# Norms of the differential attention: transposed on TensorE and stored as rows of 128 queries

## The chip, the cores and the metric

The kernel runs on one core of a Trainium2 chip. The metric is the device time of one execution in microseconds (us); three runs of the kernel before gave 2115.82, 2119.69 and 2121.97, so the median is 2119.69 us.

A core has five engines with a queue of instructions each: PE (TensorE, matrix products and transposes), DVE (VectorE), ACT (ScalarE), POOL (GpSimd) and SP (SyncE, which here only issues transfers). An engine works through its queue in order. They meet through semaphores: an instruction whose input isn't ready waits, and what is queued behind it on its engine waits with it.

## The reference

One layer is computed for two sequences (1024 and 2048 tokens): a modulated projection, a windowed attention (half A), a differential attention (half B), an output projection and a layer norm. The change concerns the norm of half B, an RMS norm over the 128 elements of each head:

```python
def rms_norm(x, w):
    xf = x.astype(jnp.float32)
    y = xf * lax.rsqrt(jnp.mean(jnp.square(xf), -1, keepdims=True) + SUBLN_EPS) * w.astype(jnp.float32)
    return y.astype(x.dtype)

def diff_attention(q, k, v, lq1, lk1, lq2, lk2, subln_w, rel_bias, lambda_init):
    ...
        p = jax.nn.softmax(logits + bias[None, :, None], axis=-1)
        w = p[:, :, 0] - lam * p[:, :, 1]
        return jnp.einsum('bhqk,bkhe->bqhe', w.astype(vh.dtype), vh)
    ...
    o = rms_norm(o, subln_w) * (1.0 - lambda_init)
```

For each of 4 heads and each query there is one number 1/sqrt(mean square + eps). The output projection needs it beside the head's output.

## The kernel before

The stages overlap: projections (50 to 1142 us), windowed attention among them (668 to 1045), the differential attention (its logits from 1076 to 1801), and the output stage (from 1829 to the end). The change lies in the differential attention and the first part of the output stage.

**Units, groups and slots.** The long sequence (s = 1) comes first, head by head, then the short one (s = 0). A unit is a block of queries of one head: 128 queries with all 2048 keys in the long sequence, 256 queries with 1024 keys in the short one. A group is 256 queries: two units of the long sequence, one unit of the short one. There are 80 units and 48 groups (32 long, 16 short), numbered from 0 here. `slot(n)` writes the work of one time step n, in four steps j = 0 to 3. In each step PE gets, in this order: four matmuls of logits of unit n (L826), six matmuls of values of an older group (L882 to L884), four transposes of the probabilities of unit n - 3 (L864). In one step of a slot `square_sum` (j = 1) adds two transposes (L897).

**What happens to logits.** DVE adds the bias and takes the minimum (L831), ACT takes the exponential with a sum (L839), DVE forms the factor of the second softmax (L841, L844), POOL scales one of the two rows (L848, two instructions a unit) and adds the other (L850, two). This combined row is what PE transposes three slots later; ACT and DVE copy the transposed block out of PSUM as a high and a low part (L866, L867). The PSUM blocks for transposes are two buffers named `tp`, used in turn.

**The norm.** `square_sum(g)` transposes a group's output (L897), ACT squares and sums it (L899), DVE adds eps times the squared sum of the softmax (L903), POOL raises it to the power -1/2 (L905). The result is `f[:, 4:6]`: 128 partitions (queries) by 2 blocks. A small function `store` is put on the list `stores`; it writes these 256 numbers to the row `frow[s][h, ...]` in device memory, one element from each of 128 partitions, twice. One `store` is taken from the list in each step while n < N = 80, and only in step j = 0 after that. In the output stage `load_rest` reads `frow` back with one row for all 128 partitions (L1024), and POOL multiplies the heads' outputs with it (L1034).

**What sets the order.** In the differential attention only PE's queue is written by hand (`manual_schedule(engines={PE})`): it is the order of the code in `slot`. The queues of the other engines are set by a scheduler at build time. In the output stage all queues are in the order of the code. W (L757, L759) is the bias of a head: it is loaded by SP and widened by two POOL instructions a head ahead of its use.

Of the kernel before, what the change touches and what calls it, by code (L numbers as in the profile page):

```python
# [11 lines left out]
F32 = mybir.dt.float32  # L12
# [8 lines left out]
P = 128  # L21
# [46 lines left out]
def hybrid_layer(ctx, tc, x_prompt, x_sample, c_prompt, c_sample, w_in, w_out, w_ada, b_ada, ln_g, ln_b,  # L68
                 attn_sink, lambda_q1, lambda_k1, lambda_q2, lambda_k2, subln_w, rel_bias, oh, eye,
                 y_prompt, y_sample):  # L70
    nc = tc.nc
# [3 lines left out]
    def pool(stack, name, bufs=1, space=None, side=None):  # L75
        if space is None:
            return stack.enter_context(tc.tile_pool(name=name, bufs=bufs, side=side, reuse_waits="tile"))
        if space == DRAM:
            return stack.enter_context(tc.tile_pool(name=name, bufs=bufs, space=space))
        return stack.enter_context(tc.tile_pool(name=name, bufs=bufs, space=space, side=side, reuse_waits="tile"))  # L80
# [6 lines left out]
    def tp():  # L87
        return ps_tp.tile([P, 512], F32, tag="tp", name="tp")
# [4 lines left out]
    def dt_(shape, name):  # L93
        return dram.tile(shape, F32, name=name, tag=name)
# [15 lines left out]
    frow = [dt_([HB, S], f"frow{s}") for s, S in enumerate(SEQS)]  # L110
    tbl = dt_([HA + HB, P, NREL], "tbl")

    ident = const.tile([P, P], F32, name="ident")
# [274 lines left out]
    def fill(n):  # L388
        for _ in range(n):
            next(steps, None)  # L390
# [316 lines left out]
    class Views:  # L707
# [5 lines left out]
        def next(self):  # L713
            if len(self.made) < self.count:
                self.made.append(self.make())
            self.n += 1
            return self.made[(self.n - 1) % self.count]

    SMAX = max(SEQS)
    QG = 256  # L720
# [6 lines left out]
    for s in (1, 0):  # L727
        T = SEQS[s] // P
        for h in range(HB):
            for i in range(0, T, 2):  # L730
                g = len(groups_of)
                n = len(units)
# [6 lines left out]
    N = len(units)  # L739
# [5 lines left out]
    st, lst = ExitStack(), ExitStack()  # L745
# [40 lines left out]
    def prefetch(n, j):  # L786

        s, h, i, g = units[n]
        if j == 1:
            for u in units[n + 1:n + (3 if n >= EARLY - 1 else 2)]:  # L790
                if u[3] == asked[0] + 1 and (u[0] == 0 or u[3] == units[n + 1][3]):
                    load_queries(u[3])
        if n in staged and j == 2:
            stage(staged[n])
        if i == (4 if s else 2) and j == 2 and (s, h) != units[-1][:2]:
            load_head(*next_head[s, h])
        if n + 1 < N and units[n + 1][2] == 0 and j == 3:
            load_keys(*units[n + 1][:2], range(2, SEQS[units[n + 1][0]] // CH))
# [53 lines left out]
    def transpose(n, j):  # L852
        s, h, i, g = units[n]
        b, kq = (i % 2, j) if s else divmod(j, 2)
        qs = slice(b * P, (b + 1) * P)
        if j == i == 0:
            load_values(s, h)
        if b == 0:
            groups_[g]["PT"].append((pt_p.tile([P, 4, QG], F32R, tag="pth", name="pth"),
                                     pt_p.tile([P, 4, QG], F32R, tag="ptl", name="ptl")))  # L860
        H, L = groups_[g]["PT"][kq]
        pt = tp()
        for c in range(4):
            nc.tensor.transpose(pt[:, c * P:(c + 1) * P], rows[n][0][:, (j * 4 + c) * P:(j * 4 + c + 1) * P], ident)  # L864
        p3 = pt.rearrange("p (j q) -> p j q", j=4)
        nc.scalar.copy(H[:, :, qs], p3)  # L866
        nc.vector.tensor_tensor(out=L[:, :, qs], in0=p3, in1=H[:, :, qs].bitcast(F32), op=ALU.subtract)  # L867
        if j == 3:
            del rows[n]

    def values(g, piece):
        s, h, i = groups_of[g]
        T = SEQS[s] // P
        G = groups_[g]
        Vt = heads[s, h][2]
        if piece == 0:
            G["O"] = ac()
        a = G["O"][:, :QG]
        for kb in range(piece * 2, piece * 2 + 2):
            kq, c = divmod(kb, 4)  # L880
            H, L = G["PT"][kq]
            nc.tensor.matmul(a, lhsT=Vt[kq][:, 0, c, :], rhs=H[:, c, :], start=(kb == 0), stop=False)  # L882
            nc.tensor.matmul(a, lhsT=Vt[kq][:, 0, c, :], rhs=L[:, c, :], start=False, stop=False)  # L883
            nc.tensor.matmul(a, lhsT=Vt[kq][:, 1, c, :], rhs=H[:, c, :], start=False, stop=(kb == T - 1))  # L884
        if piece == T // 2 - 1:
            osb = e_p.tile([P, QG], F32, tag="osb", name="osb")
            nc.scalar.copy(osb, a)
            (nc.sync if now[0] < N else nc.scalar).dma_start(out=OT[s][h][:, i * P:i * P + QG], in_=osb)
            G["osb"] = osb

    def square_sum(g):
        s, h, i = groups_of[g]
        G = groups_[g]
        ss = st_p.tile([P, 2], F32, tag="ss", name="ss")
        ot = [G["O"][:, QG + b * P:QG + (b + 1) * P] for b in range(2)]
        for b in range(2):
            nc.tensor.transpose(ot[b], G["osb"][:, b * P:(b + 1) * P], ident)  # L897
        for b in range(2):
            nc.scalar.activation(ot[b], ot[b], AF.Square, accum_out=ss[:, b:b + 1])  # L899
        f = st_p.tile([P, 6], F32, tag="f", name="f")  # L900
        nc.scalar.activation(f[:, 0:2], G["s0"], AF.Square, scale=EPS ** 0.5)
        for b in range(2):
            nc.vector.tensor_scalar(out=f[:, 2 + b:3 + b], in0=ss[:, b:b + 1], scalar1=1.0 / P,  # L903
                                    scalar2=f[:, b:b + 1], op0=ALU.mult, op1=ALU.add)
        nc.gpsimd.tensor_tensor(out=f[:, 4:6], in0=f[:, 2:4], in1=mhalf, op=ALU.pow)  # L905
        del groups_[g]

        def store():
            nc.sync.dma_start(out=frow[s][h, i * P:i * P + QG].rearrange("(b p) -> p b", p=P), in_=f[:, 4:6])

        stores.append(store)

    now, stores = [0], []

    def slot(n, extra, other=None):
        now[0] = n
        for j in range(4):
            if extra:
                fill(extra)
            if n < N:  # L920
                logits(n, j)
                prefetch(n, j)
            for g, piece in values_at.get(n, ()):
                if piece % 4 == j:
                    values(g, piece)
            if 0 <= n - LAG < N:
                transpose(n - LAG, j)
            if j == 1 and n in sums_at:
                square_sum(sums_at[n])
            if stores and (n < N or j == 0):  # L930
                stores.pop(0)()
            if other is not None:
                next(other, None)

    st_p = pool(st, "stat", 8, side="right")
    for r in (k_p, q_p, wb_p, r1_p, r0_p):
        r.open(st, "right")
    ps_lg.open(lst, space=PSUM)
    with tc.manual_schedule(engines={PE}):
        for n in range(EARLY):  # L940
            slot(n, 5)
        project_until(2, 13)
    pst.close()
    pt_p = pool(st, "pt", 7)
    v_p = pool(st, "vq", 5)
    e_p = pool(st, "e", 2)
    for r in (r0_p, r1_p, wb_p, k_p, q_p):
        r.open(st)
    ps_lg.open(lst, space=PSUM)
# [199 lines left out]
    with tc.manual_schedule(engines={PE}):  # L1149
        for n in range(EARLY, N):  # L1150
            slot(n, 0)
# [3 lines left out]
    with tc.manual_schedule(engines=ENGINES):  # L1155
        for n in range(N, max(sums_at) + 1):
            slot(n, 0, other)
        for store in stores:
            store()
        for _ in other:  # L1160
            pass
# [27 lines left out]
```

## Time and profile before

| | us |
|---|---|
| median of 3 runs | 2119.69 |
| the profiled execution's own time | 2119.7 |
| its span, first to last instruction | 2117.9 |
| PE busy | 2065.7 (98%) |
| DVE busy | 1299.6 (61%) |
| POOL busy | 1150.9 (54%) |
| ACT busy | 1039.7 (49%) |
| mean granted clock of PE | 0.994 of full |

The shares are means over stages with different limits, so the stage of the change is read by itself below. "Busy" of PE is a modelled figure: consecutive matmuls overlap, and the spacing of their starts tells what one costs. In the page's last section the store of the norms is `frow<-f`, 48 issues of 1.0 KB.

### The profile page before, as it was taken

Reading aid. Unit: us, or ns where it says so; the run is one execution under the profiler, and the core shown is the slowest. Engines: PE = TensorE matmul, PEld = TensorE weight load, DVE = VectorE, ACT = ScalarE, POOL = GpSimd, SP = SyncE. Lnnn points to the kernel's source line nnn. Section 1 sums busy time; section 2 is a strip of 40 time slices with the busy share of each in tenths; the row PEclk is TensorE's granted clock in tenths of the full one; section 3 lists DMA queues with packets and bytes.
Section 4 is the critical chain, followed back from the end, with each engine's and each line's share of the span. In section 5 each row is a group of like instructions: output and inputs, shape, how many; then the busy total and the mean of one; then the engine's idle time right before and its main releaser. Section 6 shows DMA issues by size and latency. Waiting matters only on the chain.

```text
span 2117.9 us, 32626 instructions
## 1 busy us (share of the span) xinstructions
PE 2065.7 (98%) x11597; PEld 1776.0 (84%) x11597; DVE 1299.6 (61%) x2536; ACT 1039.7 (49%) x2022; POOL 1150.9 (54%) x830
## 2 busy tenths in 40 slices
PE   7999999999999999999999999999999998799998
PEld 4777898888988888888897999999999988688886
DVE  6334224222225777777654999999999988555555
ACT  5211113011015767777623777777777887522221
POOL 3213213212224344334353889898898889577774
PEclk9999999999999999999999999999999999899999
DMA  9685635435538868778454133132231496767763
GB/s 274 183 289 156 188 121 169 131 124 134 154 118 225 207 166 217 203 198 210 131 164 146 48 91 78 39 104 58 82 78 47 114 158 87 164 157 194 197 196 103
DMA packets 340203, 312.46 MB, mean 148 GB/s; under 512 B 32086, under 2 KB 296950, under 8 KB 339656
## 3 DMA queue, kind: packets, MB, share of 16 engines
q1 hardware_dynamic: 339320, 309.72, 54.4%
q8 instruction: 92, 1.51, 0.4%
q14 instruction: 71, 0.58, 0.2%
q10 hardware_dynamic: 720, 0.66, 0.1%
HBM read 212.70 MB, written 97.60 MB: 147 GB/s over the span
## 4 chain that ended last, share of the span: by engine, by line
PE 86%; DMA 7%; DVE 3%; POOL 2%; issue 1%; ACT 1%; SPq 1%; DVEq 0%; POOLq 0%; ACTq 0%
PE lg L826 13%; PE pj L187 12%; PE pj L188 12%; PE pj L189 12%; PE tp L864 6%; PE po L1069 4%; PE po L1071 4%; PE po L1070 4%; PE ac L884 3%; PE ac L883 3%; PE ac L882 3%; PE lgA L608 3%; PE tp L644 3%; PE ac L636 2%; DMA Q<-qb 1%; PE ac L635 1%
## 5 line engine op out<-in xcount | busy, mean ns | idle before, releaser
L187 PE MATMUL pj<-uH,wH 128*128 128x512 f32 x1040 | 418.4, 402 | 4.7 <-DVE gg L258 4.7
L189 PE MATMUL pj<-uH,wL 128*128 128x512 f32 x1040 | 407.5, 392 | 0.0
L218 POOL TENSOR_TENSOR wL<-wr,wH 128x1024 fp32r<-128x1024 f32 x74 | 181.8, 2459 | 415.0 <-DVE wH L216 374.1
L188 PE MATMUL pj<-uL,wH 128*128 128x512 f32 x1040 | 407.0, 391 | 0.0
L826 PE MATMUL lg<-kt,Q 128*128 128x512 f32 x1280 | 376.4, 416 | 9.2 <-DMA Q<-qb 6.2
L850 POOL TENSOR_TENSOR l<-l,l 128x1024 f32<-128x1024 f32 x160 | 382.9, 2414 | 1.2
L839 ACT ACTIVATE l<-l,nm 128x2048 f32<-128x2048 f32 (+1 forms) x192 | 330.9, 1723 | 19.0 <-DVE nm L831 18.9
L826 PEld LDWEIGHTS lg<-kt,Q 128*128 128x128 f32 x1280 | 217.6, 190 | 40.7 <-issue 6.7
L831 DVE CUSTOM_DVE_ANT_0 l<-lg,W 128x1024 f32<-128x1024 f32 x192 | 233.4, 1215 | 11.6 <-PE lg L826 8.7
L866 ACT CAST pth<-tp 128x512 fp32r<-128x512 f32 x320 | 186.0, 581 | 108.2 <-PE tp L864 97.1
L189 PEld LDWEIGHTS pj<-uH,wL 128*128 128x128 f32 x1040 | 195.5, 188 | 42.5
L187 PEld LDWEIGHTS pj<-uH,wH 128*128 128x128 f32 x1040 | 195.9, 188 | 37.6 <-DVE gg L258 5.6
L848 POOL TENSOR_SCALAR l<-l,s 128x1024 f32<-128x1024 f32 x160 | 178.8, 1130 | 82.3 <-PE lg L826 45.4
L867 DVE TENSOR_TENSOR ptl<-tp,pth 128x512 fp32r<-128x512 f32 x320 | 209.2, 685 | 21.9 <-ACT pth L866 20.5
L188 PEld LDWEIGHTS pj<-uL,wH 128*128 128x128 f32 x1040 | 196.3, 189 | 31.0
L864 PE MATMUL tp<-ident,l 128*128 128x128 f32 x1280 | 193.6, 274 | 7.1 <-DVE ptl L867 7.1
L623 POOL TENSOR_SCALAR l<-l,rcA 128x384 f32<-128x384 f32 (+1 forms) x144 | 81.0, 581 | 190.7 <-DVE rcA L617 97.2
L884 PE MATMUL ac<-pth,vt 128*128 128x256 f32 x640 | 182.3, 285 | 0.0
L883 PE MATMUL ac<-ptl,vt 128*128 128x256 f32 x640 | 181.6, 284 | 0.0
L882 PE MATMUL ac<-pth,vt 128*128 128x256 f32 x640 | 181.4, 283 | 0.0
L831 DVE CUSTOM_DVE_ANT_0 l<-lg,W,nm 128x1024 f32<-128x1024 f32 x128 | 164.0, 1282 | 23.4 <-PE lg L826 16.1
L864 PEld LDWEIGHTS tp<-ident,l 128*128 128x128 f32 x1280 | 149.4, 141 | 9.4 <-DVE ptl L867 6.3
(207 smaller groups left out, 4023.3 us busy)
## 6 DMA issues: line engine op xcount, KB each, us to landing
wr<-in_w_in SPq DMA_DIRECT2D x39, 1024.0 KB
KAt<-ka SPq DMA_DIRECT2D x40, 384.0 KB
QAt<-qa SPq DMA_DIRECT2D x24, 512.0 KB
kt<-kb SPq DMA_DIRECT2D x24, 512.0 KB
Q<-qb SPq DMA_DIRECT2D x48, 256.0 KB
Q<-qb SPq DMA_DIRECT2D x96, 128.0 KB
vt<-vb SPq DMA_DIRECT2D x48, 256.0 KB
wa<-in_w_ada SPq DMA_DIRECT2D x32, 256.0 KB
```

The source lines that it names most:

```text
L187: nc.tensor.matmul(acc, lhsT=a(k), rhs=b(k), start=(k == 0), stop=False)
L188: nc.tensor.matmul(acc, lhsT=a(k), rhs=bl(k), start=False, stop=False)
L189: nc.tensor.matmul(acc, lhsT=al(k), rhs=b(k), start=False, stop=(k == KC - 1))
L826: nc.tensor.matmul(L[:, c * CH:(c + 1) * CH], lhsT=G["Q"][:, v, m, b * P:(b + 1) * P], rhs=Kt[kt0 + c][:, m, :], start=(v == 0), stop=(v = ...
L831: nc.vector.tensor_tensor_reduce(out=half, in0=L, in1=W[:, off:off + 1024], scale=1.0, scalar=nm[:, m, 0:1] if s and hf else 3e38, op0=ALU ...
L839: nc.scalar.activation(e, e, AF.Exp, bias=nm[:, m, hf:hf + 1], scale=-1.0, accum_out=sums)
L850: nc.gpsimd.tensor_tensor(out=row[:, cs], in0=row[:, cs], in1=rows[n][1][:, cs], op=ALU.add)
L864: nc.tensor.transpose(pt[:, c * P:(c + 1) * P], rows[n][0][:, (j * 4 + c) * P:(j * 4 + c + 1) * P], ident)
L867: nc.vector.tensor_tensor(out=L[:, :, qs], in0=p3, in1=H[:, :, qs].bitcast(F32), op=ALU.subtract)
L882: nc.tensor.matmul(a, lhsT=Vt[kq][:, 0, c, :], rhs=H[:, c, :], start=(kb == 0), stop=False)
L883: nc.tensor.matmul(a, lhsT=Vt[kq][:, 0, c, :], rhs=L[:, c, :], start=False, stop=False)
L884: nc.tensor.matmul(a, lhsT=Vt[kq][:, 1, c, :], rhs=H[:, c, :], start=False, stop=(kb == T - 1))
```

## The change

`store` no longer sends `f[:, 4:6]` from 128 partitions. It takes a `tp` buffer, lets PE transpose the 128x2 numbers into 2 rows of 128 (line 911 of the changed kernel), lets ACT copy them to a tile `fr` (line 913), and sends these two rows (line 914). `fr` has one buffer, in a pool that is opened after the projections. The buffers of the pool `stat` go from 8 to 7. `store` is now taken from the list in step j = 0 only, in all slots.

```diff
         def store():
-            nc.sync.dma_start(out=frow[s][h, i * P:i * P + QG].rearrange("(b p) -> p b", p=P), in_=f[:, 4:6])
+
+            pf = tp()
+            nc.tensor.transpose(pf[0:2, 0:P], f[:, 4:6], ident)
+            fr = f_p.tile([2, P], F32, name="fr")
+            nc.scalar.copy(fr, pf[0:2, 0:P])
+            nc.sync.dma_start(out=frow[s][h, i * P:i * P + QG].rearrange("(b p) -> b p", p=P), in_=fr)
...
-            if stores and (n < N or j == 0):
+            if stores and j == 0:
                 stores.pop(0)()
...
-    st_p = pool(st, "stat", 8, side="right")
+    st_p = pool(st, "stat", 7, side="right")
...
+    f_p = pool(st, "fr", 1)
```

PE's queue at step j = 0 of a slot in the long sequence, before (`l` is the row of combined probabilities, `f` the norms, `pth` and `vt` probabilities and values):

```order
L884 MATMUL ac<-pth,vt 128x256
L864 MATMUL tp<-ident,l_10920 128x128 x4
L826 MATMUL lg<-kt,Q 128x512 x4
L882 MATMUL ac<-pth,vt 128x256
L883 MATMUL ac<-ptl,vt 128x256
```

The same place of PE's queue now:

```order
L884 MATMUL ac<-pth,vt 128x256
L864 MATMUL tp<-ident,l_10923 128x128 x4
L911 MATMUL tp<-ident,f 2x128
L826 MATMUL lg<-kt,Q 128x512 x4
L882 MATMUL ac<-pth,vt 128x256
L883 MATMUL ac<-ptl,vt 128x256
```

The new transpose stands between the transposes of step 0 and the logits of step 1, three steps after the L897 of its group; 48 such rows are added to PE's queue, each waits for POOL's L905, and nothing else moves there.

DVE's queue of the same slot, before (L831 reduces logits, `nm` is its second result; L867 writes the low part of a transposed block and frees its `tp` buffer):

```order
L831 ISA l_11176,nm<-lg,W 128x1024
L831 ISA nm 128x1
L844 TENSOR_SCALAR s_11062<-s0g,s_11062,neglam 128x1
L831 ISA l_11176,nm<-lg,W,nm 128x1024
L831 ISA nm 128x1
L867 TENSOR_TENSOR ptl<-tp,pth 128x4x128 x2
L831 ISA l_11217,nm<-lg,W 128x1024
```

The same place of DVE's queue now:

```order
L831 ISA l_11178,nm<-lg,W 128x1024
L831 ISA nm 128x1
L844 TENSOR_SCALAR s_11065<-s0g,s_11065,neglam 128x1
L867 TENSOR_TENSOR ptl<-tp,pth 128x4x128
L831 ISA l_11178,nm<-lg,W,nm 128x1024
L831 ISA nm 128x1
L867 TENSOR_TENSOR ptl<-tp,pth 128x4x128
L831 ISA l_11224,nm<-lg,W 128x1024
```

The first L867 of a pair has moved ahead of a reduction L831, in the slots with a new transpose (30 of them). ACT gets 48 copies (line 913), each right behind L901 in the long sequence; POOL's and SP's queues keep their order around L905 and the store.

## Rows read from the trace of the kernel before

**Rows 1.** Busy time by stretch: us, busy time (count) per engine, granted clock, DMA.
```profile
1180.00:1700.00 520.00, 520.00 (x3516) 476.08 (x3515) 483.16 (x936) 414.11 (x702) 456.68 (x286) 1.00 0.29 76
1700.00:1790.00 90.00, 84.37 (x572) 76.73 (x570) 78.84 (x179) 76.31 (x174) 80.46 (x54) 1.00 0.83 127
1790.00:1850.00 60.00, 46.57 (x275) 41.67 (x276) 35.08 (x61) 34.29 (x89) 37.82 (x28) 0.86 0.63 140
```

**Rows 2.** Timeline of PE, two steps: start, duration, engine, line, operation, count.
```profile
1411.57 1.18 PE L826 MATMUL lg<-kt,Q 128*128 128x512 f32 x4
...
1413.65 1.17 PE L826 MATMUL lg<-kt,Q 128*128 128x512 f32 x4
...
1415.80 0.38 PE L897 MATMUL ac<-ident,osb 128*128 128x128 f32 x2
1415.94 0.48 PE L826 MATMUL lg<-kt,Q 128*128 128x512 f32 x1
```

**Rows 3.** Timeline of POOL and PE: group 0, then group 27.
```profile
1178.64 2.22 POOL L848 TENSOR_SCALAR l<-l,s 128x1024 f32<-128x1024 f32 x2 [0.82 <-DVE s L844]
...
1185.55 0.72 POOL L905 TENSOR_TENSOR f<-f,mhalf 128x2 f32<-128x2 f32 x1
...
1186.02 1.18 PE L826 MATMUL lg<-kt,Q 128*128 128x512 f32 x4
...
1641.00 0.70 POOL L905 TENSOR_TENSOR f<-f,mhalf 128x2 f32<-128x2 f32 x1
...
1641.44 0.72 PE L826 MATMUL lg<-kt,Q 128*128 128x512 f32 x2
```

**Rows 4.** Timeline of PE and POOL at two heads' changes: groups 5 and 29.
```profile
1270.44 1.19 PE L826 MATMUL lg<-kt,Q 128*128 128x512 f32 x4
...
1273.38 0.70 POOL L905 TENSOR_TENSOR f<-f,mhalf 128x2 f32<-128x2 f32 x1
...
1675.17 1.17 PE L826 MATMUL lg<-kt,Q 128*128 128x512 f32 x4
...
1678.46 0.71 POOL L905 TENSOR_TENSOR f<-f,mhalf 128x2 f32<-128x2 f32 x1
```

**Rows 5.** Timeline of PE and POOL in the short sequence: groups 31 and 34.
```profile
1708.87 1.19 PE L826 MATMUL lg<-kt,Q 128*128 128x512 f32 x4
...
1711.28 0.72 POOL L905 TENSOR_TENSOR f<-f,mhalf 128x2 f32<-128x2 f32 x1
...
1734.49 1.18 PE L826 MATMUL lg<-kt,Q 128*128 128x512 f32 x4
...
1740.79 2.06 POOL L759 TENSOR_SCALAR W<-W 128x1024 f32<-128x1024 f32 x2 [8.63 <-DMA W<-tbl]
...
1745.18 0.70 POOL L905 TENSOR_TENSOR f<-f,mhalf 128x2 f32<-128x2 f32 x1
```

**Rows 6.** A wait of PE (timeline; brackets: idle before, releaser) and the step behind it (stretch).
```profile
1791.58 2.04 PE L826 MATMUL lg<-kt,Q 128*128 128x512 f32 x4 [5.02 <-DMA Q<-qb]
...
1791.58:1795.17 3.59, 3.59 (x14) 3.23 (x15) 1.09 (x2) 1.98 (x4) 3.51 (x4) 0.53 0.17 39
```

**Rows 7.** Stretch in which only one old store of norms is under way.
```profile
1408.20:1408.90 0.70, 0.70 (x7) 0.66 (x6) 0.70 (x2) 0.70 (x2) 0.70 (x2) 1.00 0.21 2
```

**Rows 8.** Timeline of PE and POOL in the output stage (group 46), and a piece of the chain.
```profile
1826.09 13.72 DMA frow<-f
...
1845.90 0.51 PE L897 MATMUL ac<-ident,osb 128*128 128x128 f32 x2 [3.22 <-ACT osb L887]
...
1846.88 0.69 POOL L905 TENSOR_TENSOR f<-f,mhalf 128x2 f32<-128x2 f32 x1
```

**Rows 9.** Timeline of PE and DVE: transposes of a step 1, and the subtraction behind them.
```profile
1423.90 0.60 PE L864 MATMUL tp<-ident,l 128*128 128x128 f32 x4
...
1424.60 1.28 DVE L867 TENSOR_TENSOR ptl<-tp,pth 128x512 fp32r<-128x512 f32 x2
```

**Rows 10.** Groups of instructions by line, whole span: busy, mean ns.
```profile
L864 PE MATMUL tp<-ident,l 128*128 128x128 f32 x1280 | 193.6, 274 | 7.1 <-DVE ptl L867 7.1
```

## The prediction

> **What bounds the kernel now.** I read the stretches first. From 1180 to 1700 us, nearly the whole long sequence, PE is busy 520.00 of 520.00 us at full clock; in the short sequence 84.37 of 90, in the overlap with the output stage 46.57 of 60 [rows 1]. So in the stage of the change everything that PE issues, and every wait of PE, is added to the span, and there is no wait of PE to be won before 1700. Second I read PE's timeline for the rhythm: a step starts with the logits, and their starts lie 2.08 us apart (1411.57 to 1413.65); with two extra transposes the step takes 2.29 [rows 2]. Third, POOL's timeline: when is a group's `f` ready, and where would PE stand then.
>
> **Old stores.** 48 transfers of 256 elements go. What one costs the transfer engines shows where nothing else runs: a share of 0.21 over 0.70 us, 0.15 us of all sixteen [rows 7], 7 us in 48. PE did not wait for them in the long sequence. I count them at nothing there and come back to them for the end.
> The Trainium skill, "DMA: Bandwidth & Descriptors", section "Specifications", speaks for the change: it asks for at least 512 B a transfer, since below that the engine reads, modifies and writes. The trace has its small packets at 0.15 us a store; the rule's slow case isn't seen here, and it is weighed as the rival that forecasts a gain.
>
> **New transposes.** PE's spacing grew by 0.21 us for two transposes, so one costs 0.105 [rows 2]; 48 cost 5.0 us. (The mean duration of 274 ns [rows 10] is that of overlapping instructions.)
> The Trainium skill, "TensorE: Matmul & The Clock Gate", section "Part 4: PE-mode transpose", gives about 275 ns in a kernel. As a duration the trace agrees; as a price it would make 13 us of these 5.
>
> **The new wait.** This is the main term. The order shows the new transpose between the transposes of step 0 and the logits of step 1. It needs `f`, the last of a chain: logits of the slot before, DVE, ACT, DVE, two L848, two L850, L905. Its place on PE is where the next L826 starts now.
> - Group 0: L905 ends at 1185.55 + 0.72 = 1186.27, PE's place is 1186.02: 0.25 us late. Group 27: 1641.70 against 1641.44: 0.26 late [rows 3]. 24 of the first 28 groups look like this (0.24 to 0.30). POOL stood idle 0.82 us before this chain, until DVE's factor came [rows 3], so it hangs on PE's own logits and a stop of PE does not bring it forward: the wait returns with each group. Queued behind the waiting transpose are the logits, so DVE, ACT and POOL all start later; nothing is made good. A group costs 0.25 of waiting, 0.105 of transpose and the restart, where the weights of the next logits can't be loaded ahead: 0.05 to 0.25. I take 0.45.
> - Where a head's W is widened, POOL is behind: group 5 is 1273.38 + 0.70 - 1270.44 = 3.64 late, group 29 is 4.0 late [rows 4]; there are four such groups, the two between at 2.18 and 3.85. Together 13.7. Here POOL works without a gap, so PE's stop lets it catch up, and the groups right after (6, 22, 30, now 1.3 to 1.7 late) fall back to the usual 0.45.
> - Short sequence: POOL has work all the time. Group 31 is 1711.28 + 0.72 - 1708.87 = 3.1 late [rows 5]; part of that is the backlog that the stop at 29 has already paid: 1.7 to 3.1, I take 2.4. Group 34 stands behind W, for which POOL waited 8.63 us: f ends at 1745.88, PE's place is 1734.49, 11.4 late [rows 5]; less what 31 has cost, 9.0. Groups 35 to 39 are up to 10.5 late in this trace, but by the same backlog, so they cost only their transposes.
> - Clock: after the wait of 5.02 us PE's clock was granted at 0.53 in the next 3.59 us, the level of 1.2 GHz for nearly all of it, and the step took 3.59 instead of 2.08: 1.5 us [rows 2, 6]. Four waits (5, 21, 29, 34) are of that kind: 6.0; with 13 and second stretches up to 9.
>
> **Buffers.** The new block takes one of two `tp` buffers, so the transposes of step 1 need the buffer of step 0 back after one step, not two. Before, the two subtractions of a pair start at 1424.60, so the first is done at about 1425.24, while the transposes of step 1 start at 1423.90: 1.3 too late [rows 9]. The order has moved this subtraction ahead of a reduction (1.2 us), and PE comes 0.45 later: I cost it at nothing. Without that cover it is 1.3 a group. The copy on ACT stands behind L901, where ACT waits for PE anyway; `fr` is free a slot earlier; the 7 buffers of `stat` hold the 6 groups on the way and the new one.
>
> **The end.** Against the change: group 46's f ends at 1847.57, and PE, whose own wait there ended at 1845.90 [rows 8], would come to it earlier: 1.7 plus the three matmuls that it did before that wait, 2.4 us. For it: the chain holds 13.72 us of one old store [rows 8], under other loads, and PE is idle 13.4 us of these 60 [rows 1]; shorter stores may take a part, and the 5.02 us that PE waited for Q [rows 6], with the slow step behind it (6.5 in all), may go because transfers run on while PE stands at 34. I take -5.0 for Q (0 to -6.5) and nothing net for the rest (+4 to -8).
>
> **Sum,** against the profiled execution's 2119.7 (span 2117.9 and 1.8 around it), which is the median of the runs: 27 usual waits (24, and three after heads) x 0.45 = 12.2 (10.8 to 16.5); heads 13.7 and four transposes with restart 0.8; 17 other transposes 1.8; group 31 2.4; group 34 9.0 (8.3 to 11.4); clock 6.0 (4.5 to 9); Q -5.0; end 0. That is +40.9, **2161 us**; all low ends give 2146, all high ends 2180.
>
> **Rivals.**
> - Small stores were the brake: without them SP's queue and the loads in the crowded stretches run freely, and PE doesn't wait since POOL's f comes early enough. It decides if f is ready at PE's place. Then 5.0 is paid, 6.5 (Q) and up to the 13.4 idle at the end come back: 2120 + 5 - 15 = 2110. For it: 13.72 us of a store in the chain. Against: SP issued the old store right after f, so the end of L905 is real, and PE's place is before it.
> - Same result: the waits are paid, but the two gains at the end are at their best and PE's waits shorter: about 2120.
> - Waits mostly absorbed: the engines behind PE catch up while it stands, so that only heads and 34 remain, at two thirds: 5.0 + 9 + 6 + 3 - 5 = +18, 2138. Against it speaks POOL's idle time ahead of the usual chain.
> - The buffers bind: the subtraction comes late in spite of its new place, 1.3 x 32 = 42 more: 2203. For it: DVE is busy 483 of 520 us [rows 1]. Against: it has moved, and PE comes later.
>
> **How the numbers follow.** Forecast (2146 to 2180) 0.70; absorbed 0.11; buffers 0.10; gain 0.05; same 0.04. The range leaves out the gain, the same and the farther half of the buffers: 2132 to 2194. A measurement of this kernel can tell about 0.3% from no change, 6.4 us; so faster (below 2113) 0.05, same 0.04, slower 0.91.
>
> **What would show it.** In the changed profile the new transpose is a line with 48 instructions, and the idle time before it is put down to POOL L905: about 0.25 us in most groups, 2 to 4 in four, 8 to 11 in one, some 35 us together, on PE's weight load or its matmul. The logits' step with it takes about 2.5 instead of 2.08. PE's busy share from 1180 on is below 1, with half clock after the long waits. Waits of PE L864 for DVE L867 in step 1 would show the buffers; no idle time before the new line would make the prediction wrong altogether, and a gain would show as less idle time of PE after 1790.

## The result, and the profile after

The changed kernel takes 2138.93 us (median of 6 runs, 2136.06 to 2142.07) against 2120.59 us (median of 6) for the kernel before. The ratio is 1.0087, interval 1.0070 to 1.0104: slower by 18.3 us. The direction was forecast, the size was not: the forecast was 2161, 40.9 us more than before.

The profiled execution of the changed kernel has a span of 2139.7 us, 21.8 more than that of before, and 4.3 of these do not belong to the change. The group of the logits' matmuls by line (min/median/max ns, first and last start in us) shows it; first before, then after:

```profile
L826 PE MATMUL lg<-kt,Q x1280: 387/395/763, 1076.2 to 1800.3; 128*128 128x512 f32 x183
```

```profile
L826 PE MATMUL lg<-kt,Q x1280: 387/397/775, 1080.5 to 1820.5; 128*128 128x512 f32 x183
```

The first logits start 4.3 us later, in a stretch without a single new instruction. I therefore measure from the first to the last logits: 724.1 us before, 740.0 after, so the change costs 15.9 there, and 1.6 more from the last logits to the end (317.6 and 319.2). This "logits stretch" compares the kernels below; the start varies between them.

The stretches answer to [rows 1] (same columns). They stand at the same times, though the changed kernel is at slightly earlier work in each.

```profile
1180.00:1700.00 520.00, 508.39 (x3407) 459.15 (x3405) 468.12 (x898) 402.88 (x695) 440.49 (x275) 1.00 0.23 70
1700.00:1790.00 90.00, 88.19 (x588) 80.44 (x589) 79.92 (x175) 77.78 (x177) 82.87 (x56) 0.98 0.47 139
1790.00:1850.00 60.00, 52.99 (x362) 48.23 (x361) 49.26 (x100) 49.83 (x121) 47.13 (x32) 0.94 0.42 124
```

In the long sequence PE has lost its full 520. In the short sequence it is busier than before (88.19 for 84.37). Look at the transfer engines there: a busy share of 0.47 moves 139 GB/s, where before 0.83 moved 127. Transfers have become cheaper.

The usual group, timeline of all engines, answers to [rows 3]:

```profile
1208.04 0.27 PE L911 MATMUL tp<-ident,f 128*2 128x128 f32 x1
...
1224.49 0.70 POOL L905 TENSOR_TENSOR f<-f,mhalf 128x2 f32<-128x2 f32 x1
...
1225.24 0.08 PEld L911 LDWEIGHTS tp<-ident,f 128*2 128x2 f32 x1 [0.35 <-POOL f L905]
1225.25 0.27 PE L911 MATMUL tp<-ident,f 128*2 128x128 f32 x1
```

`f` ends at 1225.19 and PE takes it 0.05 later; the weight load of L911 had waited for 0.35. The L911 of the group before starts at 1208.04, so a group's two slots last 17.21, for 16.87 before ((1641.44 - 1186.02) / 27 in [rows 3]). The groups at the heads' changes, timeline of PE, answer to [rows 4]:

```profile
1279.22 0.37 PE L911 MATMUL tp<-ident,f 128*2 128x128 f32 x1 [2.43 <-POOL f L905]
...
1420.81 0.27 PE L911 MATMUL tp<-ident,f 128*2 128x128 f32 x1 [2.44 <-POOL f L905]
...
1560.64 0.27 PE L911 MATMUL tp<-ident,f 128*2 128x128 f32 x1 [2.19 <-POOL f L905]
...
1701.60 0.27 PE L911 MATMUL tp<-ident,f 128*2 128x128 f32 x1 [3.36 <-POOL f L905]
```

These waits are there as foreseen, 10.4 us together. The short sequence (groups 31 and 34, timeline) answers to [rows 5]:

```profile
1737.10 0.27 PE L911 MATMUL tp<-ident,f 128*2 128x128 f32 x1
...
1753.74 0.37 SPq L757 DMA_DIRECT2D W<-tbl  x1
...
1758.24 1.05 POOL L759 TENSOR_SCALAR W<-W 128x1024 f32<-128x1024 f32 x1 [0.35 <-DMA W<-tbl]
...
1763.39 0.27 PE L911 MATMUL tp<-ident,f 128*2 128x128 f32 x1 [0.21 <-POOL f L905]
```

This is the surprise. POOL waits 0.35 us for W instead of 8.63, and PE waits 0.21 at group 34 instead of the 9.0 of the forecast; at group 31 it doesn't wait. From the issue of W on SP to POOL's start on it 4.5 us pass; before it was 10.2 (start 1740.79, [rows 5]), with the issue here (timeline of SP before):

```profile
1730.58 0.33 SPq L757 DMA_DIRECT2D W<-tbl  x1
```

PE's waits for Q [rows 6] have left the list too. Waits of PE in the changed kernel from 1790 to 1850 and from 1850 to 1880 (us in total, times, longest):

```profile
PE tp L911 <- DVE ptl L867: 4.2, 2, 3.8
PE tp L911 <- POOL W L1021: 0.8, 1, 0.8
PE po L1075 <- ACT Q L1050: 0.7, 1, 0.7
...
PE tp L911 <- POOL f L905: 7.5, 2, 6.5
```

The last line is groups 46 and 47, in the place of PE's wait for osb [rows 8].

### The profile page after: what moved, and what is told of

Same layout as the page of the kernel before. It is cut to its first block, busy times and chain, and to the rows that moved or that the text cites. A ratio compares the mean times of both kernels' runs of the same rounds, so it can differ in the third digit from the quotient of the medians.

```text
span 2139.7 us, 32697 instructions
## 1 busy us (share of the span) xinstructions
PE 2076.0 (97%) x11645; PEld 1778.9 (83%) x11645; DVE 1302.1 (61%) x2536; ACT 1050.5 (49%) x2070; POOL 1151.5 (54%) x830
## 4 chain that ended last, share of the span: by engine, by line
PE 76%; POOL 13%; DMA 4%; DVE 2%; issue 2%; ACT 1%; SPq 1%; ACTq 0%; DVEq 0%; POOLq 0%
PE pj L187 12%; PE pj L188 12%; PE pj L189 12%; PE lg L826 9%; POOL l L850 8%; PE po L1075 4%; PE po L1076 4%; PE po L1077 4%; PE tp L864 4%; POOL l L848 3%; PE lgA L608 3%; PE tp L644 3%; PE ac L882 2%; PE ac L884 2%; PE ac L883 2%; PE ac L636 2%
## 5 line engine op out<-in xcount | busy, mean ns | idle before, releaser
L831 DVE CUSTOM_DVE_ANT_0 l<-lg,W 128x1024 f32<-128x1024 f32 x192 | 233.1, 1214 | 11.6 <-PE lg L826 11.5
L867 DVE TENSOR_TENSOR ptl<-tp,pth 128x512 fp32r<-128x512 f32 x320 | 212.1, 686 | 28.8 <-ACT pth L866 26.0
L864 PE MATMUL tp<-ident,l 128*128 128x128 f32 x1280 | 193.5, 274 | 1.6 <-DVE ptl L867 1.4
L623 POOL TENSOR_SCALAR l<-l,rcA 128x384 f32<-128x384 f32 (+1 forms) x144 | 81.4, 584 | 190.6 <-DVE rcA L617 97.2
L831 DVE CUSTOM_DVE_ANT_0 l<-lg,W,nm 128x1024 f32<-128x1024 f32 x128 | 163.8, 1280 | 24.4 <-PE lg L826 19.9
L864 PEld LDWEIGHTS tp<-ident,l 128*128 128x128 f32 x1280 | 149.0, 141 | 3.9 <-PE lg L826 1.1
```

The source lines that it names most:

```text
L831: nc.vector.tensor_tensor_reduce(out=half, in0=L, in1=W[:, off:off + 1024], scale=1.0, scalar=nm[:, m, 0:1] if s and hf else 3e38, op0=ALU ...
```

## The experiments

Theory 1, formed from these rows: the change pays for transposes and waits in the long sequence, and gets time back since the old stores, 256 single elements each, had slowed all other transfers. Theory 2: the stores don't matter, and the engines behind PE absorb the waits. The kernel before measured 2122.4, 2115.8 and 2122.8 us beside the three sets of runs, so only ratios are compared between sets, and not finely: rows_free and rows_free2, two nearly equal kernels in two sets, differ by 0.0024. The logits stretch is that of one profiled execution each, worked out from its line of logits as above. Kernels of one kind without the old stores agree in it to 0.3 us (rows_free to rows_free3; late2, late2_tail, late2_flush); those with them less well (rule_only, whose order on PE is that of before, has 726.3 for 724.1):

```
kernel            ratio    95% interval      logits stretch   last logits to end
before            1                          724.1            317.6
after             1.0087   1.0070 to 1.0104  740.0            319.2
wait_scatter      1.0169   1.0150 to 1.0188  752.3            320.5
late2             0.9977   0.9966 to 0.9988  720.1            318.2
late2_scatter     1.0089   1.0070 to 1.0109  734.8            319.8
rows_free         1.0006   0.9995 to 1.0016  714.6            318.0
rows_free2        1.0030   1.0018 to 1.0042  714.6            317.2
rows_free3        0.9967   0.9954 to 0.9979  714.6            320.7
twice             1.0608   1.0581 to 1.0636  821.3            341.5
pairs             1.0161   1.0141 to 1.0181  740.7            331.4
rule_only         1.0006   0.9994 to 1.0017  726.3            319.1
late2_tail        1.0003   0.9993 to 1.0013  719.8            319.6
late2_flush       0.9990   0.9981 to 1.0000  719.8            324.1
```

**wait_scatter**: transposes and waits kept, the old store back.

```
-            nc.sync.dma_start(out=frow[...].rearrange("(b p) -> b p", p=P), in_=fr)
+            nc.sync.dma_start(out=frow[...].rearrange("(b p) -> p b", p=P), in_=f[:, 4:6])
```

> The changed kernel with its transposes, its waits for f and its copies, but the norms go out as before, 256 single elements from 128 partitions; the copied row is not used. Theory 1 (the small stores slow the other transfers, and the row store gives that back in the short sequence): up to the short sequence as the changed kernel, some 18 us behind before; then the transfer engines are near 0.8 busy again between group 31 and 39 instead of 0.47, POOL waits several us for W ahead of group 34, PE waits for Q, and the time is 2139 + 9 to 20 = 2148 to 2159. Theory 2 (the waits of PE are worth less than forecast because the engines behind PE use them, the stores don't matter): 2139, within 4 us.

2155.21 us. PE's timeline at groups 31 and 34, then the stretch from 1700 to 1790, then POOL's waits for W from 1700 to 1800:

```profile
1733.29 0.37 PE L911 MATMUL tp<-ident,f 128*2 128x128 f32 x1 [5.05 <-POOL f L905]
...
1769.74 0.37 PE L911 MATMUL tp<-ident,f 128*2 128x128 f32 x1 [8.91 <-POOL f L905]
```

```profile
1700.00:1790.00 90.00, 76.04 (x493) 69.08 (x493) 68.10 (x150) 66.90 (x154) 67.81 (x46) 0.92 0.58 121
```

```profile
POOL W L759 <- DMA W<-tbl: 15.8, 2, 9.1
```

The wait of 9.0 that I had forecast for group 34 is there, at 8.91, as soon as the old stores are, and group 31, forecast at 2.4, waits 5.05. Only the store differs from the changed kernel (its form, and that it leaves from `f` without the copy), so it is the store that made W late. The share of 0.58 is lower than the 0.8 expected, perhaps since PE's stops spread the loads. Theory 2 falls.

**late2**: the changed kernel with the transpose two steps later.

```
-        stores.append(store)
+        stores.append((now[0], store))
...
-            if stores and j == 0:
-                stores.pop(0)()
+            if stores and n > stores[0][0] and j == 2:
+                stores.pop(0)[1]()
...
```

> The changed kernel with the new transpose two steps (some 4.2 us) later on PE, so that f is ready at every group up to the short sequence (it was 0.25 late in most groups and 3.6 to 4.0 at most). All else as in the changed kernel. Theory 1: waits of PE for f go (18.5 us listed, and the short ones of the weight load), the 48 transposes stay at 0.105 (5.0 us), the gain of the row store stays: 2120.6 + 5 - 9 = 2117 (2112 to 2121). Theory 2 (stores don't matter): 2120.6 + 5 = 2126 (2124 to 2129). A third: the transposes themselves and the buffer they take cost more than 0.105, the waits little: 2133 to 2139.

2118.25 us, as theory 1 said: well below the changed kernel, and a little below before, ratio 0.9977 with an interval that leaves out 1; its logits stretch is 4.0 us shorter than that of before. Its usual groups on PE:

```profile
1208.82 0.27 PE L911 MATMUL tp<-ident,f 128*2 128x128 f32 x1
...
1225.76 0.27 PE L911 MATMUL tp<-ident,f 128*2 128x128 f32 x1
...
1242.69 0.27 PE L911 MATMUL tp<-ident,f 128*2 128x128 f32 x1
```

16.94 and 16.93 between them. Of the 0.34 that a usual group costs the changed kernel, some 0.07 is the transpose and 0.27 the wait with its restart.

**late2_scatter**: the same with the old store (the edit of wait_scatter in late2).

> The kernel with the new transpose two steps later (2118.25 us against 2122.4 of before), but with the norms going out as 256 single elements again; the copied row is not used. It is the fourth of four: wait and row 2138.9, wait and single elements 2155.2, later and row 2118.25, this one later and single elements. Theory 1 (the single elements stall other transfers in the short sequence and at the end, whether PE waits or not): waits of PE for Q or of POOL for W return, 2118.25 + 5 to 12 = 2123 to 2130. Theory 2 (single elements cost something only where the transposes make SP or PE wait for f): 2118 within 3 us.

Ratio 1.0089 (2134.46 us beside 2115.77). That is 24 us above late2 by the ratios of the two sets, 16 by the times as they stand and 14.7 in the logits stretch: by each more than any theory had. Its trace has the old waits again, now on DVE's account (PE's waits from 1150 on):

```profile
PE tp L864 <- DVE ptl L867: 12.4, 7, 6.2
PE ac L897 <- ACT osb L887: 3.9, 1, 3.9
```

In late2 the first of these is 4.0 us, 1.4 at most. POOL waits 5.46 and 7.22 us for W in the short sequence, where in late2 it doesn't wait. Theory 1 in kind; why it costs more than forecast is not shown.

**rows_free, rows_free2, rows_free3**: no transposes and no waits, a row of other numbers in place of the norms.

```
-            nc.sync.dma_start(out=frow[...].rearrange("(b p) -> p b", p=P), in_=f[:, 4:6])
+            nc.sync.dma_start(out=frow[...].rearrange("(b p) -> b p", p=P), in_=ident[0:2, 0:P])
+            nc.sync.dma_start(out=fx[s][h, i:i + 2, :], in_=f[0:2, 4:6])
```

In rows_free2 `fx` has the size of the norms; in rows_free3 the row is `osb[0:2, 0:P]`. Lines of these kernels, and of twice and pairs, have numbers one or more higher than before.

> The kernel before, without transposes and waits, but the 256 single elements are replaced by a row of a constant (2 packets of 512 B; the norms are left out of the result) and 4 elements of f into a place of their own, so that SP still waits for f. Theory 1: the transfers are freed and nothing is paid: POOL's wait for W at group 34 falls from 8.63 us to under 3, PE's waits for Q (6.2 us) go, and the time is 2120.6 - 9 = 2112 (2106 to 2114). Theory 2: 2120.6 within 4 us, W's and Q's waits as before.

A miss: 2123.5 us, nothing gained, though its logits stretch is 9.5 us shorter. The start shows a new wait (PE, first 680 us):

```profile
PE tp L170 <- DMA x<-in_x_prompt: 6.9, 2, 4.6
```

> As the run with a row of a constant in place of the norms (no transposes, no wait), but the extra place in memory has the size of the norms' own, since that run lost 9.9 us before the first logits of the long sequence (1086.1 against 1076.2), in waits for the input x of up to 4.6 us, and won 8.5 from there to the end. Theory 1a (the new place of 1 KB moved the other arrays in memory, and that cost the start its 10 us): the start is back at 1076 to 1080 and the time is 2122.4 - 8.5 = 2114 (2110 to 2117). Theory 1b (the start's 10 us come from the changed stores themselves, or from an accident of the profile): the start stays at 1086 and the time at 2123.5. Theory 2 (the stores cost nothing): 2122 and waits for W and Q as before.

1b: the start stays long (first logits at 1086.2), so the place in memory is not the cause. On SP the likely cause can be seen (timeline of rows_free2):

```profile
40.36 8.43 SPq L910 DMA_DIRECT2D frow<-ident  x11
48.89 0.95 SPq L152 DMA_DIRECT2D x<-in_x_prompt  x2
49.89 5.11 SPq L910 DMA_DIRECT2D frow<-ident  x15
```

A constant is ready at once, so 42 of the 48 stores were put between the first loads of x, in the first 58 us; only the six of the output stage, whose order is that of the code, stayed at their place.

> The kernel before without transposes and waits; in place of the norms a row of two partitions of the attention output goes out (2 packets of 512 B, the norms are left out of the result), at the place of the old store on SP, and 4 elements of f behind it. In the two earlier runs of this kind the 48 stores of a constant stood between the first loads of x on SP, since a constant is ready at once, and the start lost 10 us; here the row is ready only with its group. Theory 1: the start is as before, and from the first logits to the end the 9 to 10 us come back that those two runs showed: 0.45% faster, ratio 0.9955 (0.994 to 0.997). Theory 2 (the start's loss was the price of something that these stores always need): ratio 1.000 to 1.003.

Ratio 0.9967, 7 us, with the start as before. Its line of logits, and the stretch from 1700 to 1790:

```profile
L827 PE MATMUL lg<-kt,Q x1280: 387/395/500, 1077.7 to 1792.3; 128*128 128x512 f32 x183
```

```profile
1700.00:1790.00 90.00, 90.00 (x613) 82.48 (x612) 85.27 (x191) 82.69 (x184) 86.44 (x58) 1.00 0.41 121
```

PE is busy 90 of 90, and 520 of 520 from 1180 to 1700. All three kernels have a logits stretch of 714.6: this is PE without stops from 1180 on. In its trace the kernel before lost 9.5 us to its small stores (rule_only 11.7). Only 7 of them show in the time of rows_free3. Its end is longer (320.7 for 317.6), in part because the stand-in's row is read from `osb`: ACT waits 3.93 and 3.33 us for these stores before it can write `osb` again. The other two have no longer end (318.0 and 317.2).

**twice and pairs**: the kernel before with a second store of the same norms, as 256 packets of 4 B (twice) or 128 of 8 B (pairs).

```
 (pairs)
+            nc.sync.dma_start(out=fx[...].rearrange("(p b) -> p b", b=2), in_=f[:, 4:6])
```

> The kernel before, with each of the 48 stores of single elements issued a second time, to a place of its own. Theory 1: twice the small packets, so the waits behind slow transfers in the short sequence and at the end grow: 2120.6 + 5 to 15 = 2126 to 2136, PE's waits for Q and POOL's for W longer than 6.2 and 8.63 us, the transfer engines' share between 1700 and 1790 us above 0.83. Theory 2: 2120.6 within 4 us.

> The kernel before, with each store of norms issued a second time to a place of its own as in the run that took 2251.6 us, but the second time as 128 packets of two neighbouring elements (8 B) and not as 256 of one (4 B). If the stall goes with the number of packets below 512 B: half of the 129 us, 2122.4 + 45 to 85 = 2167 to 2207. If it goes with the store (128 partitions, whatever its packets): about 2250. If only 4 B elements do it: 2122 to 2130.

2251.62 us (ratio 1.0608) and 2149.95 (1.0161). The longest waits of PE from 1150 on, of twice, then of pairs:

```profile
PE tp L865 <- DVE ptl L868: 39.1, 16, 10.5
PE lg L827 <- DMA Q<-qb: 32.0, 9, 9.3
PE lg L827 <- DVE nm L832: 18.7, 11, 9.0
```

```profile
PE tp L865 <- DVE ptl L868: 19.3, 11, 9.9
PE ac L898 <- ACT osb L888: 11.4, 1, 11.4
```

Theory 1 in kind, but ten times its size in twice: of the logits stretch the first 48 stores cost 9.5 us and the second 48 cost 97.2; with the end the second cost 129. In pairs the second store has half the packets, of 8 B for 4, and costs 34 us, which lies between two of the ranges (0 to 8 and 45 to 85). So the price is not one per packet. That early loads hide the first delays and leave the rest exposed would fit, but was not tried by itself. The second store of rows_free3, 2 packets of 8 B, costs PE nothing (90 of 90), so packets below 512 B are not dear when they are few. Number and size were not varied one by one.

**rule_only**: the other two lines of the change (the rule for taking stores, 7 buffers for 8) in the kernel before.

> The kernel before with the two other lines of the change alone: a store is taken only in the first step of a slot, and the pool of small numbers has 7 buffers, not 8. Transposes, copies and rows are left out. The order of PE is that of before, on SP one store of norms moves ahead of two stores of ot near the end. All theories: 2 us at most, ratio 0.999 to 1.001. If the seventh buffer or the store's place cost something, ratio above 1.0015.

1.0006, interval 0.9994 to 1.0017: nothing.

**late2_tail and late2_flush**: two attempts at the end of late2.

```
 (late2_tail)  +            if tail:   # group summed after the last logits slot
               +                nc.sync.dma_start(out=frow[...].rearrange("(b p) -> p b", p=P), in_=f[:, 4:6])
               +                return
 (late2_flush) -            if stores and n > stores[0][0] and j == 2:
               +            if stores and n - stores[0][0] >= (1 if n < N else 2) and j == 2:
```

> The kernel with the new transpose two steps later, but in the stretch where the output stage has begun (the last groups) norms go out as before, straight from f, without transpose, copy or wait. There the trace with the later transpose still shows PE idle before L911 (4.42, 0.60, 0.53, 0.44 us) and for the copy of the row (2.63, 0.63), 9 us with a clock that falls to half behind it. Theory 1: some of this comes back and a few single elements cost 0 to 3: 2118.25 - 4 = 2114 (2110 to 2117). Rival: PE in this stretch waits for DVE, ACT and the squares anyway (3.22 us for osb in the kernel before), and the single elements stall loads there: 2118 to 2122.

> The kernel with the new transpose two steps later (ratio 0.9977), and in the stretch with the output stage a slot later still, the last two behind eight steps of the output matmuls. In its trace PE waited 4.42 us for the f of the last group but one, and the clock fell to half behind that. Theory 1: this wait goes, 4 us: ratio 0.9958 (0.994 to 0.997). Rival: PE waits there for the output's own inputs (ACT Q, 0.7 to 6 us in the other kernels) and for osb as the kernel before does: 0.9977 within 0.0012.

Ratios 1.0003 and 0.9990: no gain over late2 is shown. The rivals hold in kind, though neither figure lies in its rival's range. The logits stretch is within 0.3 us of that of late2 in both. In late2_flush PE's longest wait there moves to the copy of the row:

```profile
PE tp L911 <- ACT fr L913: 6.2, 1, 6.2
```

## Why the prediction was right in direction and wrong in size

The runs split the change on the logits stretch. From PE without stops (714.6), the transposes cost 5.3 where `f` is ready (719.9, mean of late2, late2_tail and late2_flush; in late2 a wait of 0.9 is among it); putting them where `f` isn't ready costs 20.1 more (740.0); and the kernel before carried 9.5 from its small stores. 5.3 + 20.1 - 9.5 = 15.9. The 9.5 is the least certain of the three, to some 2 us. In the same parts the forecast was 5.0 for transposes, 40.9 for waits with their clock (the same figure as the whole sum, since the other two cancel), and -5.0 for Q. The direction was no luck: transposes and waits cost 25.4, far more than the stores give back. The size was wrong, and the step that failed lies in the account of the old stores.

- **The step that failed** is "Old stores": I priced a store by what the transfer engines were busy with where nothing else ran, 0.15 us [rows 7], and wrote "I count them at nothing there". For the long sequence that holds: from 1180 to 1700 us packets of 1024 B took 55 ns in the mean before and 53 in rows_free3, those of 2048 B 103 and 104. In the short sequence, which is more crowded with transfers (127 GB/s for 76, [rows 1]), it does not, and when I came back to the stores I priced only Q and the end. Their own packets are short there too; what they cost is the time of others. From the records of transfers in the traces, from 1700 to 1790 us (the windows hold somewhat different work):

```
                      4096 B packets            4 B packets
kernel            count  mean ns  median    count  mean ns
before             512     749      159      3292     15
after              384     200      159       909     10
wait_scatter       256     619      159      2416     10
late2              512     194      159       909     10
late2_scatter      512     499      159      2994     10
rows_free3         512     215      159       875     10
```

  after and wait_scatter differ in the store alone, and so do late2 and late2_scatter. The median is untouched; single packets take microseconds (over 1 us: 119 of the 512 before, 2 in late2). The rows that should have warned me were [rows 1], share 0.83 for 127 GB/s against 0.29 for 76 before it, and the 13.72 us of one store in the chain [rows 8]. Where the packets wait is not shown: nearly all go by one queue (q1 of the page before: 339320 of 340203), and no run tells a delay in that queue from one in the memory behind it.
- **The term that this mis-sized** is the short sequence: 2.4 for group 31 and 9.0 for group 34, read off POOL's wait of 8.63 for W [rows 5]. That wait was caused by the stores which the change removes, so I carried a delay of the old kernel into the new one. The two waits measured 0 and 0.2, and 5.05 and 8.91 in wait_scatter. Forecasting 11.4 for these 0.2 makes 11.2 of the 20.8 us between forecast and measured waits (40.9 and 20.1); the rest is in the terms below.
- **Q:** -5.0 forecast; PE's place moved from 28.9 us behind before at group 34 (1763.39 for 1734.49, [rows 5]) to 20.2 at the last logits (1820.5 for 1800.3), a gain of 8.7 with the transposes of that stretch already paid. The waits of 1.23 and 5.02 for Q and the slow step behind are gone, and a wait of 0.96 for DVE that hung on the late W. The first two of these in the kernel before (timeline of PE):

```profile
1746.55 0.73 PE L826 MATMUL lg<-kt,Q 128*128 128x512 f32 x2 [0.96 <-DVE nm L831]
...
1769.52 0.70 PE L826 MATMUL lg<-kt,Q 128*128 128x512 f32 x2 [1.23 <-DMA Q<-qb]
```

- **Usual waits:** 0.45 forecast, 0.34 measured; over 27 groups 9.2 for 12.2. The transpose was 0.07 of it for 0.105, and wait with restart 0.27 for some 0.35; for the restart (0.05 to 0.25) no row of before had a price. That the waits return with every group was right: late2 removes them and nothing else replaces them.
- **Heads:** 13.7 forecast, 10.4 measured. In wait_scatter the four are 1.23, 2.19, 2.03 and 2.98, so the stores are not the reason. "Here POOL works without a gap" was wrong: POOL stands idle ahead of each L759, mostly for the head's W (timeline of POOL, four lines of before, then four of after):

```profile
1259.67 2.06 POOL L759 TENSOR_SCALAR W<-W 128x1024 f32<-128x1024 f32 x2 [2.66 <-PE ac L884]
1393.12 2.06 POOL L759 TENSOR_SCALAR W<-W 128x1024 f32<-128x1024 f32 x2 [1.20 <-DMA W<-tbl]
1529.55 2.07 POOL L759 TENSOR_SCALAR W<-W 128x1024 f32<-128x1024 f32 x2 [2.91 <-DMA W<-tbl]
1664.78 2.07 POOL L759 TENSOR_SCALAR W<-W 128x1024 f32<-128x1024 f32 x2 [2.99 <-DMA W<-tbl]
...
1264.81 2.07 POOL L759 TENSOR_SCALAR W<-W 128x1024 f32<-128x1024 f32 x2 [2.10 <-DMA W<-tbl]
1406.41 2.06 POOL L759 TENSOR_SCALAR W<-W 128x1024 f32<-128x1024 f32 x2 [2.08 <-DMA W<-tbl]
1546.20 2.07 POOL L759 TENSOR_SCALAR W<-W 128x1024 f32<-128x1024 f32 x2 [1.77 <-DMA W<-tbl]
1687.21 2.07 POOL L759 TENSOR_SCALAR W<-W 128x1024 f32<-128x1024 f32 x2 [3.12 <-PE ac L884]
```

  The lateness of before (3.64, 2.18, 3.85, 4.0) is this idle time plus 0.94 to 1.01; PE's wait in the changed kernel is it plus 0.24 to 0.42. So the size of each stop follows POOL's idle time ahead of L759; why what comes on top fell stays open.
- **Clock:** 6.0 forecast for four stops (5, 21, 29, 34). It measured 2.9, since half clock followed only two: the two slots behind group 5 take 18.72 and behind 29 18.56, for the usual 17.21. At 34 there was no stop. Stretches behind the stops at groups 5, 13 and 29:

```profile
1279.50:1283.10 3.60, 3.60 (x16) 3.20 (x16) 1.29 (x2) 0.26 (x2) 3.60 (x3) 0.58 0.00 0
1421.00:1424.60 3.60, 3.60 (x25) 3.25 (x25) 2.06 (x4) 1.65 (x3) 3.60 (x3) 1.00 0.02 5
1701.90:1705.50 3.60, 3.60 (x16) 3.27 (x16) 1.23 (x2) 0.55 (x2) 3.60 (x3) 0.57 0.00 0
```

  0.58 and 0.57 are 1.2 GHz for most of the stretch, 16 matmuls where 25 fit. A stop of 2.43 was followed by it, one of 2.44 was not.
- **Buffers and end:** no wait of PE L864 for DVE L867 appears from 1180 to 1700, as costed. The end cost 1.6 for 0: PE's wait of 6.5 at group 46 was forecast at 2.4, but the 3.22 for osb [rows 8] went.

The rival "waits mostly absorbed" gave 2138, but not for its reason: more than half of the missing waits were not absorbed by engines that catch up, they had lost their cause. The rival "small stores were the brake" was right on the stores; its condition, that `f` is early enough, was wrong at the changed kernel's place on PE and is true two steps later, in late2.

The Trainium skill, "DMA: Bandwidth & Descriptors", section "Specifications", asks for at least 512 B a transfer for line rate, because below that the engine reads, modifies and writes. The runs agree that many stores below that size are dear: a second set of 48 x 256 x 4 B costs 129 us. That the dearness comes from reading and writing back no run here shows, and it falls on other transfers more than on the small ones.

## What to carry to other kernels

When a change replaces something, ask of each wait in the old trace whether the thing replaced causes it, before pricing it in the new kernel: a store of 256 single elements looks like 0.15 us where nothing else runs, and delays loads by microseconds in a crowded stretch. The sign is a transfer share that rises far more than the bytes (0.83 for 127 GB/s, where the changed kernel has 0.47 for 139). A transpose put into a saturated PE costs little by itself (5.3 us for all), but its operand must be ready at its place in the order; here a move by two steps turned 0.9% slower into 0.2% faster, the latter in one set of runs only: the two variants of late2 were at 1.0003 and 0.9990 in other sets. In an experiment, a store of a constant has no dependence and may be issued at the very start: give a stand-in the same readiness as what it replaces, and look at which buffer it holds longer.

## What the runs showed of the hardware that was not expected

- Small stores can stall other packets more than themselves: with 256 x 4 B per store, packets of 4096 B took 749 ns in the mean for 194 without them, at the same median of 159, while their own took 15 for 10. This is the short sequence, from 1700 to 1790 us; from 1180 to 1700 the same stores left the other packets of the kernel before nearly as they are without them (1024 B: 55 ns for 53).
- The cost of such stores is far from linear: in the logits stretch 9.5 us for 48 of them, 97.2 for the next 48 of 256 packets, 16.6 for the next 48 of 128 packets of 8 B.
- Of two stops of PE of 2.43 and 2.44 us one was followed by half clock and the other was not (0.58 and 1.00 in the 3.6 us behind).
